# Low parts of weight blocks made 2048 columns at a time, a fourth row pair in sevens, and modulations moved out of a matrix

## The chip, the cores and the metric

The kernel runs on one core of one Trainium2 chip. The metric is the device time of the whole program in microseconds (us), the median of several runs. A core has five engines that run on their own and wait for each other by semaphores: TensorE (PE, matrix products into the eight banks of PSUM), VectorE (DVE), ScalarE (ACT), GpSimd (POOL), and SyncE (SP), which here issues the loads.

## The reference

A trunk of two layers over 256 tokens of width 2048, all in fp32. Each layer has a token mixer and a SwiGLU feed-forward; both are fed by an RMS norm with a shift and a scale, and added back through a gate. Shift, scale and gate are columns of a product of the conditioning vector with `w_mod` (the modulations):

```python
for i in range(DEPTH):                       # 2 layers
    mod = (c_act @ w_mod[i] + b_mod[i])[:, None, :]
    sh1, sc1, g1, sh2, sc2, g2 = jnp.split(mod, 6, axis=-1)
    h = rms_norm(x, norm1_g[i]) * (1.0 + sc1) + sh1
    y = retention_mixer(h, ...) if i == 0 else short_conv_mixer(h, ...)
    x = x + g1 * y
    h = rms_norm(x, norm2_g[i]) * (1.0 + sc2) + sh2
    a, b = jnp.split(h @ ffn_w_in[i], 2, axis=-1)      # 2048 -> 2 x 5632
    x = x + g2 * ((jax.nn.silu(a) * b) @ ffn_w_out[i]) # 5632 -> 2048
return rms_norm(x, final_g)
```

## The kernel before

**Products in parts.** An fp32 weight `w` and an activation are each written as a high and a low part that TensorE takes at full rate, and a product is three matmuls (high x high, high x low, low x high). ScalarE makes the high part by a cast (L419), VectorE the low part by subtracting the high part from the raw weight (L422).

**Blocks, pieces and places.** All weight matrices lie in one array `w_all` of 456 blocks of 128 rows x 2048 columns, in the order of their use. A block is loaded into one of four buffers `raw` (1 MB a load; the modulations' rows of `w_mod` take the same four buffers). `prepare` handles one piece of a block at a time: piece 0 and piece 1 are the two halves of 1024 columns. Each piece goes to the next of five places (`PLACES`) of 1024 columns in the tiles `hi` and `lo`; they are used in turn, so a cast into a place must wait until TensorE has read what stood there five places ago. `take` hands weights to the matmuls and calls `prepare` whenever a place has been used up and `fits()` says that there is room.

**Sevens.** In the first matrices of the feed-forwards, eight row pairs (two rows of 128 each, one block: two rows times two groups of 512 columns) make one group of 512 x 2 output columns for 256 tokens. A plain row pair takes 24 matmuls of 512 columns. Some row pairs are done with seven products for eight (`Seven`, 21 matmuls): VectorE makes sums and differences of the block's quarters, in four pieces: piece 2 (difference of quarters into `differences`, then the low part of columns 1024 to 2047), piece 3 (low part of `differences`), piece 4 (one 512-wide difference, then the low part of columns 0 to 1023), piece 5 (one more 512-wide difference and its 512-wide low part). That is seven VectorE operations: four of 1024 columns and three of 512, and four casts. The activations of such a row pair are summed as well, once, in `made_in_sums`. At a group's end `mixed_sums` and `last_input` put the banks together on VectorE (ten operations of 512), and a transposition, called two row pairs into the next group, adds two more. `FFN_SEVEN` names the row pairs of layer 0 that are sevens, `IN_SEVEN` and `OUT_SEVEN` those of layer 1. Layer 0's matrix is used in two parts: four such groups (after some first columns), its output matrix's first rows, then six such groups and the remaining output rows.

**Modulations.** There are 160 outside the start, each one load of 1 MB and one VectorE operation of 2048 columns (L326). `paced` spreads them over the program by `plan_mod`, a list of points (units of work done so far, modulations done by then); a unit is 128 x 128 weights. The retention mixer covers units 0 to 2048 (its first 496 in a form of its own, `RET_SPANS`), layer 0's feed-forward units 2048 to 4160: first columns and four groups to 2688, output to 3008, six groups to 3776, output to 4160; the convolution mixer ends at 5184.

**Order.** TensorE's instructions stand in the order in which the code is written. VectorE's and ScalarE's are put in order by a scheduler, and each engine then runs its list strictly from first to last: an instruction that waits holds up all behind it on its engine.

Of the kernel before, what the change touches and what calls it, by code (L numbers as in the profile page):

```python
# [31 lines left out]
CHUNK = 2048  # L32
HALF = 1024
# [8 lines left out]
IN_SEVEN, OUT_SEVEN, TURNS_AT, BESIDE_CB, BESIDE_SUMS = (3, 4, 6), ((2, 4, 6, 5, 1), (2, 4, 6, 10, 8)), 2, 40, 48  # L42
LAST_TILES = 20, 24
ONE_GROUP = (1, 1)
FFN_TILES, FFN_SEVEN, FFN_TURNS = (20, 24), (2, 4, 6), 2
STORE_AT, LOAD_AT = 0, 2
LEAD_RET, LEAD_CONV, LEAD_FFN = 6, 4, 2
AHEAD = 2
# [5 lines left out]
PLACES = 5  # L54
FETCHED, PLAIN, WARM, ADDED = 2, 3, (5, 0, 0, 0, 0, 0, 0, 8), ()
# [71 lines left out]
RET_SPANS, RET_HEADS = ret_in_groups()  # L127
# [6 lines left out]
class Seven:  # L134
# [6 lines left out]
    n = 2 * DV // P  # L141
# [123 lines left out]
def trunk(ctx: ExitStack, tc: tile.TileContext, x_in, c_in, pos_in, w_mod, cols_in, gain_in, tab_in, w_all, out):  # L265
    nc = tc.nc
    const = ctx.enter_context(tc.tile_pool(name="const", bufs=1))
    work = ctx.enter_context(tc.tile_pool(name="work", bufs=2))
    wpool = ctx.enter_context(tc.tile_pool(name="wpool", bufs=1))
# [22 lines left out]
    at = [0]  # L292
# [49 lines left out]
    n_mod = len(todo)  # L342
    todo.reverse()
    first = RET_SPANS[0].n * FIRST_KS
    early = sum(g.n * len(g.ks) for g in RET_SPANS)
    plan_mod = [(early, 0), (1024, 28), (1984, 72), (2688, 80), (3008, 96), (3776, 102), (5184, n_mod)]
    units, allowed = [0], [0.0]

    def paced(n):
# [19 lines left out]
    ready, place, raws, fetched, n_fetched = [], [None], [], {}, [0]  # L369
    in_seven, n = set(), 0  # L370
# [2 lines left out]
            in_seven.add(n // CHUNK)  # L373
        n += g.n * P * len(g.ks)

    pieces = [(i, p) for i in range(PLAIN, w_all.shape[0]) for p in ((2, 3, 4, 5) if i in in_seven else (0, 1))]

    def fetch():
        raw = wpool.tile([P, CHUNK], F32, tag="raw", name=name("raw"), bufs=RAW_BUFS)
# [13 lines left out]
    def prepare(between=None):  # L393
        if prepared[0] == len(pieces):
            return
        index, piece = pieces[prepared[0]]
        prepared[0] += 1
        if piece in (0, 2, 6):
            raws[:] = [next_raw(index)]
            while first <= units[0] < early and len(fetched) < RAW_BUFS - 1 and n_fetched[0] < w_all.shape[0]:  # L400
                fetch()
        whole = raws[0]
        b = [whole[:, i : i + DV] for i in range(0, CHUNK, DV)]
        raw = whole[:, :HALF] if piece in (0, 4) else whole[:, HALF:] if piece < 6 else whole
        if piece == 2:
            nc.vector.tensor_tensor(differences[0], whole[:, DV : 3 * DV], whole[:, : 2 * DV], op=ALU.subtract)
        elif piece == 3:
            raw = differences[0]
        elif piece == 4:
            nc.vector.tensor_tensor(b[1], b[2], differences[0][:, :DV], op=ALU.subtract)  # L410
        elif piece == 5:
            nc.vector.tensor_tensor(b[3], b[3], b[1], op=ALU.subtract)
            raw = b[3]
        width, at = raw.shape[1], HALF * (taken_places[0] % PLACES)
        taken_places[0] += -(-width // HALF)
        hi, lo = [t[:, at : at + width] for t in split_weights]
        steps = [slice(i, min(i + HALF, width)) for i in range(0, width, HALF)]
        for o in steps:
            nc.scalar.copy(hi[:, o], raw[:, o])  # L419
        if between:  # L420
            between()
        nc.vector.tensor_tensor(lo, raw, hi.bitcast(F32), op=ALU.subtract)  # L422
        ready.extend((hi[:, o], lo[:, o], o.stop - o.start) for o in steps)

    taken_places = [0]
    split_weights = [
        wpool.tile([P, PLACES * HALF], F32R, tag=tag, name=tag) for tag in ("hi", "lo")
    ]
    prepared = [0]

# [291 lines left out]
    with ExitStack() as inner:  # L722
# [64 lines left out]
        with tc.tile_pool(name="start", bufs=1) as sp:  # L787
# [59 lines left out]
            with tc.manual_schedule(engines={mybir.EngineType.DVE, mybir.EngineType.Activation}):  # L847
# [35 lines left out]
                sums = bank()[:, 0, :]  # L883
# [436 lines left out]
    with tc.tile_pool(name="ffn", bufs=1) as fpool:  # L1320
        h = rows_at(EARLIER)
        own.update(pool=fpool, sums={}, turns=FFN_TURNS)
        first_mid = paired(fpool, max(FFN_TILES))[: FFN_TILES[0] // 2]
        differences[0] = fpool.tile([P, 2 * DV], F32, tag="differences", name="differences")
        own["extra"] = [fpool.tile([P, DV], F32, tag=f"extra{i}", name=f"extra{i}") for i in range(2)]
        for part in range(2):
            n = FFN_TILES[part] // 2
            mid = paired(fpool, FFN_TILES[part]) if part else first_mid
            if not part:
                first_rows(FFN_FIRSTS, mid[-2:], 0, 1)  # L1330
                made_in_sums(FFN_SEVEN, [
                    fpool.tile([P, 2, P], F32R, tag=f"sums{i}", name=f"sums{i}") for i in range(6)
                ] + [tmp("u", (P, 2, P), F32R, bufs=3) for _ in range(3)])
# [13 lines left out]
    for i, g in enumerate(CONV_IN):  # L1347
        pending += [sums(g)] if i else normed(acc, 1, 0, g)
        while len(pending) >= 3:
# [3 lines left out]
            b, c, u = pb(tmp("bsum", pool=mpool, bufs=2)), pc(), pu()  # L1353
# [205 lines left out]
```

## Time and profile before

| | before |
|---|---|
| time, median of 3 runs (lowest to highest) | 2562.66 us (2562.12 to 2562.8) |
| span of the profiled execution, first to last instruction | 2558.4 us |
| granted TensorE clock | 0.998 |
| busy PE / VectorE / ScalarE | 2539.3 / 2354.7 / 1351.2 us |
| `lo` subtractions (L422) | 1062, of which 78 have 512 columns, the others 1024 |
| modulations outside the start (L326) | 160 |
| HBM read | 685.11 MB |

The profile is one execution; the page gives its span, and no time of its own beyond that. The span is 4.3 us below the median of the runs. Lines name kernel.py's lines of the kernel before. In a timeline row stand the start, the length (both us from the span's start), engine, line, operation, output <- inputs, shapes, and in brackets how long the engine was idle before and what ended that. Successive VectorE operations may overlap by their ends, so a step from start to start is shorter than the length.

### The profile page before, as it was taken

What the parts mean: (1) busy time and instruction counts of PE and PEld (TensorE: products, weight loads), DVE (VectorE), ACT (ScalarE), POOL (GpSimd) and SP (SyncE); (2) the same over time, 40 slices, a digit from 0 to 9 for tenths busy, and PEclk for the clock granted to TensorE, in tenths of its full rate; (3) what the DMA queues carried; (4) which work ended last, traced back from release to release, by engine and by line L of the source; (5) the groups of instructions that cost most, each with busy time, mean ns of one, the idle gap of its engine ahead of it and who ended that gap; (6) DMA issues with size and microseconds to landing.
All of it is one profiled execution on the core that took longest, in us unless ns stands there. A gap on an engine that the chain in (4) does not pass through costs nothing.

```text
span 2558.4 us, 34761 instructions
## 1 busy us (share of the span) xinstructions
PE 2539.3 (99%) x13237; PEld 2181.4 (85%) x13237; DVE 2354.7 (92%) x2968; ACT 1351.2 (53%) x1799; POOL 179.3 (7%) x234
## 2 busy tenths in 40 slices
PE   8999999999999999999999999999999999999998
PEld 7898888888889888888888898888998888888886
DVE  7989999898899999889999899888989999999998
ACT  5544543454456554345555454445566555555554
POOL 0000121011110001000000012000000000000001
PEclk9999999999999999999999999999999999999999
DMA  9987888879875667866667879888846465555653
GB/s 399 396 329 264 319 317 340 333 287 331 325 281 213 237 234 293 336 249 228 216 228 299 328 270 344 314 306 309 323 158 215 180 230 214 181 214 183 228 183 146
DMA packets 96695, 689.47 MB, mean 269 GB/s; under 512 B 10744, under 2 KB 12168, under 8 KB 13456
## 3 DMA queue, kind: packets, MB, share of 16 engines
q1 hardware_dynamic: 96528, 687.25, 72.2%
q8 instruction: 103, 1.69, 0.3%
q14 instruction: 64, 0.52, 0.1%
HBM read 685.11 MB, written 2.11 MB: 269 GB/s over the span
## 4 chain that ended last, share of the span: by engine, by line
PE 94%; DVE 3%; DMA 1%; ACT 1%; issue 1%; POOL 0%; SPq 0%; ACTq 0%; POOLq 0%; DVEq 0%
PE bank L472 22%; PE bank L487 17%; PE bank L485 17%; PE bank L486 17%; PE bank L475 11%; DVE lo L422 1%; PE bank L667 1%; PE bank L669 1%; PE bank L668 1%; PE bank L536 1%; PE bank L535 1%; PE bank L534 1%; DVE raw L798 1%; DMA raw<-w_all 1%; PE bank L1290 1%; PE bank L1067 1%
## 5 line engine op out<-in xcount | busy, mean ns | idle before, releaser
L419 ACT CAST hi<-raw 128x1024 fp32r<-128x1024 f32 (+1 forms) x984 | 991.1, 1019 | 936.7 <-PE bank L487 325.1
L422 DVE TENSOR_TENSOR lo<-raw,hi 128x1024 fp32r<-128x1024 f32 (+1 forms) x984 | 1143.3, 1179 | 125.6 <-ACT hi L419 116.7
L485 PE MATMUL bank<-hi,h 128*128 128x512 f32 x1540 | 602.9, 391 | 0.0
L487 PE MATMUL bank<-hi,h 128*128 128x512 f32 x1540 | 601.2, 390 | 0.0
L486 PE MATMUL bank<-lo,h 128*128 128x512 f32 x1540 | 601.1, 390 | 0.0
L326 DVE SCALAR_TENSOR_TENSOR raw<-raw,cb 128x2048 f32<-128x2048 f32 x160 | 365.4, 2285 | 8.2 <-DMA raw<-w_mod 8.0
L472 PE MATMUL bank<-h,hi 128*128 128x512 f32 x1012 | 352.8, 392 | 0.0
L487 PEld LDWEIGHTS bank<-hi,h 128*128 128x128 f32 x1540 | 289.4, 188 | 61.0
L485 PEld LDWEIGHTS bank<-hi,h 128*128 128x128 f32 x1540 | 289.6, 188 | 58.1
L486 PEld LDWEIGHTS bank<-lo,h 128*128 128x128 f32 x1540 | 289.7, 188 | 57.5
L472 PE MATMUL bank<-mid,hi 128*128 128x512 f32 x920 | 319.4, 391 | 0.0
L475 PE MATMUL bank<-h,lo 128*128 128x256 f32 x1012 | 285.0, 282 | 0.0
L475 PE MATMUL bank<-mid,lo 128*128 128x256 f32 x920 | 259.7, 282 | 0.0
L472 PEld LDWEIGHTS bank<-h,hi 128*128 128x128 f32 x1012 | 190.1, 188 | 40.3
L472 PEld LDWEIGHTS bank<-mid,hi 128*128 128x128 f32 x920 | 172.9, 188 | 35.6
L475 PEld LDWEIGHTS bank<-h,lo 128*128 128x128 f32 x1012 | 191.6, 189 | 0.5
L475 PEld LDWEIGHTS bank<-mid,lo 128*128 128x128 f32 x920 | 174.3, 189 | 0.1
L472 PE MATMUL bank<-rm,hi 128*128 128x512 f32 x496 | 172.5, 391 | 0.0
L475 PE MATMUL bank<-rm,lo 128*128 128x256 f32 x496 | 140.0, 282 | 0.0
L487 PE MATMUL bank<-hi,mid 128*128 128x512 f32 x284 | 110.9, 391 | 0.0
L485 PE MATMUL bank<-hi,mid 128*128 128x512 f32 x284 | 110.9, 391 | 0.0
L486 PE MATMUL bank<-lo,mid 128*128 128x512 f32 x284 | 110.7, 390 | 0.0
(300 smaller groups left out, 3344.2 us busy)
## 6 DMA issues: line engine op xcount, KB each, us to landing
raw<-w_all SPq DMA_DIRECT2D x456, 1024.0 KB, 5.0
raw<-w_mod SPq DMA_DIRECT2D x192, 1024.0 KB, 6.1
x<-x_in SPq DMA_DIRECT2D x4, 512.0 KB, 5.3
out<-xt SPq DMA_DIRECT2D x4, 512.0 KB, 3.0
decay<-tab_in SPq DMA_DIRECT2D x8, 128.0 KB, 4.9
x<-gate_row SPq DMA_DIRECT2D x2, 512.0 KB, 4.6
last_gain<-gain_in SPq DMA_DIRECT2D x1, 1024.0 KB
cols<-cols_in SPq DMA_DIRECT2D x1, 152.0 KB, 8.2
```

The costliest lines, as they stand in the source:

```text
L326: nc.vector.scalar_tensor_tensor(raw, raw, 1.0, cb, op0=ALU.mult, op1=ALU.mult, accum_out=total)
L419: nc.scalar.copy(hi[:, o], raw[:, o])
L422: nc.vector.tensor_tensor(lo, raw, hi.bitcast(F32), op=ALU.subtract)
L472: nc.tensor.matmul(pt, hi, h, start=fresh and k == g.ks[0], stop=False, skip_group_check=True)
L475: nc.tensor.matmul(pt[:, 1, :], lo, h[:, 0, :], start=False, stop=last and k == g.ks[-1], skip_group_check=True)
L485: nc.tensor.matmul(o, hi, w_hi, start=first, stop=False)
L486: nc.tensor.matmul(o, hi, w_lo, start=False, stop=False)
L487: nc.tensor.matmul(o, lo, w_hi, start=False, stop=last)
L534: nc.tensor.matmul(pt, hi, h[:, 0, :], start=first, stop=False, skip_group_check=True)
L535: nc.tensor.matmul(pt, hi, h[:, 1, :], start=False, stop=False, skip_group_check=True)
L536: nc.tensor.matmul(pt, lo, h[:, 0, :], start=False, stop=last, skip_group_check=True)
L667: nc.tensor.matmul(pt, hi, high, start=k == 0, stop=False, skip_group_check=True)
```

## The change

Three things change.

1. Blocks that are neither in sevens nor among the first 31 blocks (and the one behind them) are prepared as one piece, number 6: two casts of 1024 columns into two places as before, and then one subtraction of 2048 columns for both. Where the two places are the last and the first, the second lies four places back, and the operation takes them with a negative step. There are 336 such blocks. `fits()` lets such a piece be prepared only when two of the five places are free.
2. `FFN_SEVEN` goes from row pairs (2, 4, 6) to (2, 3, 5, 6). Ten groups each have one more seven, and `made_in_sums` makes a fourth set of sums.
3. `plan_mod`: 32, not 28, modulations by unit 1024; 78, not 72, by 1984; still 80 by 2688 and 96 by 3008; then 96, not 102, by 3776: none during the six groups, and six more after them.

```diff
-FFN_TILES, FFN_SEVEN, FFN_TURNS = (20, 24), (2, 4, 6), 2
+FFN_TILES, FFN_SEVEN, FFN_TURNS = (20, 24), (2, 3, 5, 6), 2
...
-    plan_mod = [(early, 0), (1024, 28), (1984, 72), (2688, 80), (3008, 96), (3776, 102), (5184, n_mod)]
+    plan_mod = [(early, 0), (1024, 32), (1984, 78), (2688, 80), (3008, 96), (3776, 96), (5184, n_mod)]
...
-    pieces = [(i, p) for i in range(PLAIN, w_all.shape[0]) for p in ((2, 3, 4, 5) if i in in_seven else (0, 1))]
+    apart = range(sum(g.n * len(g.ks) for g in RET_SPANS) * P // CHUNK + 1)
+    pieces = [(i, p) for i in range(PLAIN, w_all.shape[0]) for p in ((2, 3, 4, 5) if i in in_seven else (0, 1) if i in apart else (6,))]
...
-        nc.vector.tensor_tensor(lo, raw, hi.bitcast(F32), op=ALU.subtract)
-        ready.extend((hi[:, o], lo[:, o], o.stop - o.start) for o in steps)
+        if n == 1:
+            nc.vector.tensor_tensor(los[0], raw, his[0].bitcast(F32), op=ALU.subtract)
+        else:
+            step = 1 if at + 1 < PLACES else 1 - PLACES
+            end = None if at + 2 * step < 0 else at + 2 * step
+            hi, lo = [t[:, at:end:step, :] for t in split_weights]
+            raw = raw.rearrange("p (a b) -> p a b", a=2)
+            nc.vector.tensor_tensor(lo, raw, hi.bitcast(F32), op=ALU.subtract)
+        ready.extend((hi, lo, v.shape[1]) for hi, lo, v in zip(his, los, rows))
...
-        wpool.tile([P, PLACES * HALF], F32R, tag=tag, name=tag) for tag in ("hi", "lo")
+        wpool.tile([P, PLACES, HALF], F32R, tag=tag, name=tag) for tag in ("hi", "lo")
...
-                    fpool.tile([P, 2, P], F32R, tag=f"sums{i}", name=f"sums{i}") for i in range(6)
+                    fpool.tile([P, 2, P], F32R, tag=f"sums{i}", name=f"sums{i}") for i in range(9)
```

The lists below are of the second of the six groups. A block's name `raw_N` stands for one row pair. Before, `raw_9787` is row pair 3 (plain), `raw_9805` row pair 4 (seven), `raw_9851` row pair 5 (plain), `raw_9869` row pair 6 (seven). ScalarE before:

```order
L1294 CAST mid_9413<-bank_9776 128x2x256
L419 CAST hi<-raw_9787 128x1024
L419 CAST hi<-raw_9805 128x1024
L419 CAST hi<-differences 128x1024
L419 CAST hi<-raw_9805 128x1024
L419 CAST hi<-raw_9805 128x512
L419 CAST hi<-raw_9851 128x1024 x2
L419 CAST hi<-raw_9869 128x1024
```

After, `raw_9675` is row pair 3 (now a seven), `raw_9715` row pair 4 (plain), `raw_9726` row pair 5 (seven), `raw_9772` row pair 6 (seven), `raw_9812` row pair 7. ScalarE after, the same stretch:

```order
L1303 CAST mid_9306<-bank_9664 128x2x256
L421 CAST hi<-differences 128x1024
L421 CAST hi<-raw_9715 128x1024
L421 CAST hi<-raw_9675 128x1024
L421 CAST hi<-raw_9675 128x512
L421 CAST hi<-raw_9715 128x1024
L421 CAST hi<-raw_9726 128x1024
```

Before, a seven's casts stand together and the next plain block's two behind them; now the plain block's first cast (`raw_9715`) stands ahead of the seven's last two (`raw_9675`). At row pairs 6 and 7 it stands ahead of the 512-wide one:

```order
L421 CAST hi<-raw_9772 128x1024
L421 CAST hi<-differences 128x1024
L421 CAST hi<-raw_9772 128x1024
L421 CAST hi<-raw_9812 128x1024
L421 CAST hi<-raw_9772 128x512
L421 CAST hi<-raw_9812 128x1024
```

Over the ten groups the first of these places occurs ten times and the second nine times; in layer 1, of 37 places where a plain block follows a seven, twice each. VectorE before, from the same group:

```order
L422 TENSOR_TENSOR lo<-raw_9805,hi 128x512
L406 TENSOR_TENSOR differences<-raw_9869 128x1024
L326 SCALAR_TENSOR_TENSOR raw_9691,msum_9693<-raw_9691,cb 128x2048
L422 TENSOR_TENSOR lo<-raw_9851,hi 128x1024 x2
L422 TENSOR_TENSOR lo<-raw_9869,hi 128x1024
```

and after:

```order
L413 TENSOR_TENSOR raw_9675<-raw_9675 128x512
L407 TENSOR_TENSOR differences<-raw_9726 128x1024
L425 TENSOR_TENSOR lo<-raw_9675,hi 128x1024
L425 TENSOR_TENSOR lo<-raw_9675,hi 128x512
L431 TENSOR_TENSOR lo<-raw_9715,hi 128x2048
L425 TENSOR_TENSOR lo<-raw_9726,hi 128x1024
```

The modulation (L326) has left the group, and the plain row pair's two low parts are one operation (L431).

More of the change, by code (lines that the diff above doesn't have):

```diff
@@ L413, in prepare @@
             raw = b[3]
[L414 to L419, printed above, removed]
+        width, at = raw.shape[1], taken_places[0] % PLACES
+        n = -(-width // HALF)
+        taken_places[0] += n
+        rows = [raw[:, i : min(i + HALF, width)] for i in range(0, width, HALF)]
+        his, los = [[t[:, (at + i) % PLACES, : v.shape[1]] for i, v in enumerate(rows)] for t in split_weights]
+        for hi, v in zip(his, rows):
+            nc.scalar.copy(hi, v)
         if between:
             between()
-        nc.vector.tensor_tensor(lo, raw, hi.bitcast(F32), op=ALU.subtract)
-        ready.extend((hi[:, o], lo[:, o], o.stop - o.start) for o in steps)
+        if n == 1:
[7 more added lines that the diff above has]
+        ready.extend((hi, lo, v.shape[1]) for hi, lo, v in zip(his, los, rows))
     taken_places = [0]
     split_weights = [
-        wpool.tile([P, PLACES * HALF], F32R, tag=tag, name=tag) for tag in ("hi", "lo")
+        wpool.tile([P, PLACES, HALF], F32R, tag=tag, name=tag) for tag in ("hi", "lo")
     ]
```

## The prediction

> **What bounds the kernel now.** I read the page first (busy time, then the chain that ended last), then the groups of instructions by shape, the windows by stage, and last the timelines of single row pairs.
>
> ```profile
> span 2558.4 us, 34761 instructions
> PE 2539.3 (99%) x13237; PEld 2181.4 (85%) x13237; DVE 2354.7 (92%) x2968; ACT 1351.2 (53%) x1799; POOL 179.3 (7%) x234
> PE 94%; DVE 3%; DMA 1%; ACT 1%; issue 1%; POOL 0%; SPq 0%; ACTq 0%; POOLq 0%; DVEq 0%
> L485 PE MATMUL bank<-hi,h 128*128 128x512 f32 x1540 | 602.9, 391 | 0.0
> L422 DVE TENSOR_TENSOR lo<-raw,hi 128x1024 fp32r<-128x1024 f32 x906 | 1096.0, 1221 | 124.8 <-ACT hi L419 115.9 <-PE bank L472 2.5
> L326 DVE SCALAR_TENSOR_TENSOR raw<-raw,cb 128x2048 f32<-128x2048 f32 x160 | 365.4, 2285 | 8.2 <-DMA raw<-w_mod 8.0
> L419 ACT CAST hi<-raw 128x1024 fp32r<-128x1024 f32 x906 | 946.3, 1053 | 899.5 <-PE bank L487 324.8 <-PE bank L472 291.4 <-DMA raw<-w_all 109.6
> L419 ACT CAST hi<-raw 128x512 fp32r<-128x512 f32 x78 | 48.5, 621 | 37.3 <-DVE raw L412 36.1 <-PE bank L487 0.3 <-DVE x L406 0.3
> ```
>
> TensorE carries 94% of the chain and its matmuls of 512 columns waited 0.0 us, so its count of matmuls is worth time one for one. VectorE is second at 92%. ScalarE's casts idle 899.5 us, mostly until PE has let go of a place. In the stages that the change touches (the windows' columns are the stretch, its length, then each engine's busy time):
>
> ```profile
> 200.00:300.00 100.00, 99.46 (x510) 84.68 (x509) 99.13 (x137) 51.17 (x76) 11.79 (x14) 1.00 0.79 297
> 300.00:400.00 100.00, 100.00 (x533) 86.40 (x532) 95.30 (x130) 44.47 (x64) 21.65 (x26) 1.00 0.84 319
> 988.00:1099.00 111.00, 111.00 (x645) 98.66 (x644) 98.12 (x109) 43.76 (x44) 9.00 (x17) 1.00 0.87 330
> 1141.60:1184.20 42.60, 42.60 (x193) 35.18 (x192) 40.43 (x46) 24.28 (x27) 1.11 (x1) 1.00 0.62 223
> ```
>
> The last row is one group of the first feed-forward matrix (eight row pairs, three in sevens, one modulation): PE 42.6 of 42.6 us, VectorE 40.4. The two rows at the top are the retention heads, the third a feed-forward output.
>
> The row that decides is how a seven meets the next plain block. PE, ScalarE and VectorE at such a meeting (start, length):
>
> ```profile
> 1110.61 0.39 PE L487 MATMUL bank<-hi,h 128*128 128x512 f32 x1
> 1110.84 0.39 PE L485 MATMUL bank<-hi,u 128*128 128x512 f32 x1
> ...
> 1113.78 0.39 PE L486 MATMUL bank<-lo,h 128*128 128x512 f32 x1
> ...
> 1115.14 0.39 PE L486 MATMUL bank<-lo,h 128*128 128x512 f32 x1
> ...
> 1115.82 0.39 PE L486 MATMUL bank<-lo,h 128*128 128x512 f32 x1
> 1108.61 1.05 ACT L419 CAST hi<-raw 128x1024 fp32r<-128x1024 f32 x1 [0.68 <-DVE raw L410]
> 1111.08 2.52 ACT L419 CAST hi<-raw 128x1024 fp32r<-128x1024 f32 x3 [1.43 <-PE bank L487]
> 1110.15 1.23 DVE L422 TENSOR_TENSOR lo<-raw,hi 128x1024 fp32r<-128x1024 f32 x1
> 1112.17 2.96 DVE L422 TENSOR_TENSOR lo<-raw,hi 128x1024 fp32r<-128x1024 f32 x3 [0.79 <-ACT hi L419]
> ```
>
> PE begins a seven at s = 1110.84. ScalarE had stood idle 1.43 us at the cast of the next plain block's first place, which is the fifth after the last place of the row pair in front; it starts at 1111.08, s+0.24. The seven's own last cast (512 wide) stands behind it in ScalarE's queue. VectorE, idle 0.79 us for the same cast, makes the plain low part first (to 1113.39, read at 1115.82), then the 512 one (to 1113.99, read at 1115.14: 1.15 us to spare). The seven's third piece is read at 1113.78 = s+2.94; here it stood ahead of the waiting cast, its low part ended at 1111.38, and nothing was lost.
>
> **Durations.** PE's step is 0.2265 us (20 from 1110.61 to 1115.14). VectorE's steps, back to back:
>
> ```profile
> 1163.92 2.28 DVE L326 SCALAR_TENSOR_TENSOR raw<-raw,cb 128x2048 f32<-128x2048 f32 x1
> 1166.13 0.08 DVE L326 DVE_READ_ACCUMULATOR raw<-raw,cb 128x1 f32 x1
> 1166.13 3.49 DVE L422 TENSOR_TENSOR lo<-raw,hi 128x1024 fp32r<-128x1024 f32 x3
> 1143.02 0.68 DVE L1276 TENSOR_TENSOR u<-bank,u 128x512 f32<-128x512 f32 x1
> 1143.61 0.68 DVE L1276 TENSOR_TENSOR extra<-bank,extra 128x512 f32<-128x512 f32 x1
> 1152.56 1.03 PE L1290 MATMUL bank<-tab,extra 128*128 128x128 f32 x8
> 1195.20 1.04 PE L1290 MATMUL bank<-tab,extra 128*128 128x128 f32 x8
> ```
>
> Three of 1024 last 3.49, so a step is (3.49-1.22)/2 = 1.135; 512 steps 0.60; 2048 steps 2.21 (nearest row: the modulation's, the only 2048-wide operation). A wide low part has no row. 0.60 and 1.135 make 0.535 for 512 columns and 0.065 fixed, so 2048 take 2.205; the modulation says 2.21, and the ends are 2.14 (no fixed part) and 2.27 (two of 1024). I take a step of 2.20 and a length of 2.28. It saves 0.07 us a block, 336 blocks, 23 us of VectorE, hidden behind PE wherever PE is the bound: 0.
>
> **The fourth seven.** Ten groups each lose 24-21 = 3 matmuls: 30 x 0.2265 = 6.8 us of PE, on the path: **-6.8**. VectorE's work in a group becomes 16 operations of 1024 (18.2), 24 of 512 with the twelve of the group's end (14.4), four wide (8.8) = 41.4 us without waits; PE's is 42.64-0.68 = 41.96 (a group repeats after 1195.20-1152.56 = 42.64). Taking the group's modulation out (2.2) is what makes this fit; it alone buys nothing, as PE hid it. So VectorE has 0.5 us of room in 42.
>
> **What the order does at row pairs 3 and 4.** In the changed order ScalarE casts the first place of plain row pair 4 *ahead of* the third and fourth piece of the seven of row pair 3 (all ten groups). That place is freed when PE ends row pair 2, at s of row pair 3. With the measured chain: cast s+0.24, the third piece's cast 0.95 later, s+1.19 to 2.24, its low part s+2.28 to 3.50. PE wants it at s+2.94, so it waits 0.6 us. Then the 512 low part (s+3.42) and the wide one, s+4.02 to 6.30 (its second cast is done at s+3.7). PE wants that at s+4.79+0.23+0.60 = 5.62: 0.7 more. Together 1.35 us a group, x10 = **+13.5**. Behind the waiting cast stand the next casts, behind those every low part of VectorE, which has no room to make it up.
>
> **Wide after a seven elsewhere.** From the second layer, the seven at 2285.48 and the plain block after it:
>
> ```profile
> 2285.48 0.39 PE L485 MATMUL bank<-hi,u 128*128 128x512 f32 x1
> 2290.47 0.39 PE L486 MATMUL bank<-lo,h 128*128 128x512 f32 x1
> 2285.72 1.05 ACT L419 CAST hi<-raw 128x1024 fp32r<-128x1024 f32 x1 [1.13 <-issue]
> 2287.09 1.06 ACT L419 CAST hi<-raw 128x1024 fp32r<-128x1024 f32 x1 [0.32 <-PE bank L487]
> 2286.81 3.95 DVE L422 TENSOR_TENSOR lo<-raw,hi 128x1024 fp32r<-128x1024 f32 x3 [0.88 <-ACT hi L419]
> ```
>
> Now the first low part ends at 2288.03, 2.44 before it is read (2290.47). A wide one needs both casts, 2288.15, and ends at 2290.47: nothing left, some 0.06 us lost each time. In layer 1 the changed order has 37 such meetings: 33 plain (2.0), two with the cast ahead of the third piece (2.7), two with it ahead of the fourth (0.35 each, 0.7). At row pair 7 of the ten groups the 512 cast again stands behind the plain block's first, which puts its second cast 0.3 later: nine of 0.35 and one of 0.06, 3.2. Together **+8.6**, ends 3.4 (0.06 everywhere) and 14.
>
> **Modulations.** Six more run before the first feed-forward: 6 x 2.21 = 13.3 us of VectorE, less 97 blocks x 0.07 = 6.8 saved there. VectorE is 97% busy from 200 to 400 us by the windows. The worst lead there, in the first retention output:
>
> ```profile
> 411.42 2.35 DVE L422 TENSOR_TENSOR lo<-raw,hi 128x1024 fp32r<-128x1024 f32 x2
> 413.82 0.28 PE L475 MATMUL bank<-rm,lo 128*128 128x256 f32 x1
> 405.62 2.01 ACT L419 CAST hi<-raw 128x1024 fp32r<-128x1024 f32 x2 [2.95 <-DMA raw<-w_all]
> ```
>
> The first low part ended at 412.64, 1.2 before use; the wide form ends 1.1 later, at the edge. ScalarE stood 2.95 us for a load, so a late load is also felt about 2 us more (the second cast and the longer subtraction). Between 0 and 13; I take **+2**, nearest to the single edge that the row shows. One modulation is left in the first part's third group, and the first group makes a fourth set of sums: 0 to 4.4, **+1**, as that group loses two modulations. Six later ones go where VectorE has 12% free (98.1 of 111 in the like stage): 0. DMA counts and bytes stay; the queue only moves.
>
> Sum: -6.8+13.5+8.6+2+1 = **+18.3**. The profiled span is 2558.4, 4.3 below the median of 2562.66; the median plus the sum is **2581**.
>
> Of VectorE's steps: rows 1166.13 and 1143.02 show operations that start 0.086 us before the one in front has ended. The Trainium skill's page VectorE: DVE Perf Modes says otherwise in its section on the DRAIN: the next operation starts only when the pipe has emptied (it adds that one that is not held starts earlier). Its errata section gives an fp32 tensor_tensor (N+151)/0.96 ns, 1224 for 1024 columns; the trace's length of 1221 agrees, its step of 1135 does not. By that rule the time would be the first rival's.
>
> **Rivals.**
> *VectorE becomes the bound outright.* If operations did not overlap, a group would be 16 x 1.221 + 24 x 0.687 + 4 x 2.285 = 45.2 us against 42.64, ten times 2.5 = 25, with 9 for the rest: **2597**. The three in 3.49 us speak against it; so does a group before, whose 22 operations of 1024, 21 of 512 and one modulation would need 43.7 by lengths yet show 40.43. 0.07.
> *The waits are covered* (the other side). If the casts at row pair 3 came 0.6 us earlier, by a shorter cast or a freed place, and VectorE's 41.4 stayed under 41.96, only the 6.8 us of PE remain: **2556**. It decides where waits fall below 0.68 us a group. The third piece had such a cover before, by its place in the queue, and the 1.15 us at 1115.14 are one; nothing frees the place sooner. 0.10.
> *The mixer loses more.* The six modulations find no gaps and loads come late: +11 on top, **2592**. For it 99.13 of 100 us; against it PE's 99.46 there, and slack in most blocks. 0.10.
> *Half of the stalls.* Row pair 4 catches up, only 0.6 and 0.06 remain: -6.8+6.6+3 = +3, **2565**; VectorE's room of 0.5 would have to serve it. With less in the rest this is no change. 0.13.
>
> **How the numbers follow.** My forecast has 0.60, own range 2571 to 2592 (row pair 4 half caught up, the rest at its low ends; the rest at its high ends). Within 0.2% (5.1 us, about what a measurement tells apart) lies the half-stall case, 0.13; faster only the covered one, 0.10; the rest, 0.77, is slower. Leaving out the covered case, the range is 2563 to 2597.
>
> **What would show it.** The matmuls of L485 to L487 fall by 30 and no longer have idle 0.0; VectorE's `lo` appears 336 times as one 2048-wide operation of 2.28 us; the repeat of a feed-forward group grows from 42.6 to about 43.6; PE waits some 0.6 us for `lo` in the middle of row pair 3's seven and 0.7 at row pair 4, with ScalarE idle until PE at a cast of plain `raw` just ahead. I am wrong if the repeat is 42.0, or if VectorE is busy throughout a group and PE's waits lie all over it.

## The result and the profile after

The changed kernel takes 2606.97 us (median of 4 runs, 2604.09 to 2608.53) against 2562.39 us (2560.7 to 2562.8): a ratio of 1.0176, 95% interval 1.0161 to 1.019. It is slower, as forecast, but by 44.6 us and not by 18.3, and outside the range (2563 to 2597). The profiled execution took 2607.33 us. From its page, the span, the busy times, the chain by engine, and two groups (operation, count, busy time, mean ns, idle time in front and what ended it):

```profile
span 2605.6 us, 34376 instructions
PE 2560.5 (98%) x13207; PEld 2173.6 (83%) x13207; DVE 2371.7 (91%) x2692; ACT 1365.2 (52%) x1823; POOL 188.4 (7%) x234
PE 81%; DVE 13%; issue 4%; ACT 2%; DMA 0%; POOL 0%; ACTq 0%; POOLq 0%; DVEq 0%
L431 DVE TENSOR_TENSOR lo<-raw,hi 128x2048 fp32r<-128x2048 f32 x336 | 768.0, 2286 | 94.6 <-ACT hi L421 93.7
L495 PE MATMUL bank<-lo,h 128*128 128x512 f32 x1500 | 591.3, 394 | 16.6 <-DVE lo L425 8.6
```

PE has its 30 matmuls less. VectorE's share of the chain grew from 3% to 13% though VectorE is busy 91% of the span, not more than before: over the whole span no other engine became the bound, PE waits here and there for a low part. So the question is at which places. The table splits the span at matmuls that stand in both kernels (the first matmul of each normed product, and the transposition behind each feed-forward group); differences to before in us, one profiled execution each. "Ten groups" are the first feed-forward's four groups and, with its output rows between, the six up to the last transposition.

| kernel | mixer | first four groups | six groups | outputs, convolution | layer 1, first rows | layer 1, rest | span |
|---|---|---|---|---|---|---|---|
| before, us | 771.8 | 221.8 | 366.7 | 485.8 | 102.6 | 609.5 | 2558.4 |
| after | +14.8 | +9.8 | +6.2 | 0.0 | +1.2 | +15.2 | +47.2 |
| predicted | +2 | +5 | +6 | 0 | 0 | +5.4 | +18.3 |

The prediction's terms for the ten groups (-6.8, +13.5, 3.2, +1) make 10.9; they are parted here as four to six.

### The profile page after: what moved, and what is told of

The parts are those of the page before. It is cut to its first block, busy times and chain, and to the rows that moved or that the text cites. A ratio compares the mean times of both kernels' runs of the same rounds, so it can differ in the third digit from the quotient of the medians.

```text
span 2605.6 us, 34376 instructions
## 1 busy us (share of the span) xinstructions
PE 2560.5 (98%) x13207; PEld 2173.6 (83%) x13207; DVE 2371.7 (91%) x2692; ACT 1365.2 (52%) x1823; POOL 188.4 (7%) x234
## 4 chain that ended last, share of the span: by engine, by line
PE 81%; DVE 13%; issue 4%; ACT 2%; DMA 0%; POOL 0%; ACTq 0%; POOLq 0%; DVEq 0%
PE bank L481 20%; PE bank L495 14%; PE bank L496 14%; PE bank L494 13%; PE bank L484 11%; DVE lo L431 4%; DVE lo L425 3%; ACT hi L421 2%; PE bank L544 1%; PE bank L545 1%; PE bank L543 1%; PE bank L676 1%; PE bank L678 1%; PE bank L677 1%; DVE raw L326 1%
## 5 line engine op out<-in xcount | busy, mean ns | idle before, releaser
L431 DVE TENSOR_TENSOR lo<-raw,hi 128x2048 fp32r<-128x2048 f32 x336 | 768.0, 2286 | 94.6 <-ACT hi L421 93.7
L495 PE MATMUL bank<-lo,h 128*128 128x512 f32 x1500 | 591.3, 394 | 16.6 <-DVE lo L425 8.6
L494 PE MATMUL bank<-hi,h 128*128 128x512 f32 x1500 | 587.8, 392 | 0.7 <-ACT hi L421 0.7
L496 PE MATMUL bank<-hi,h 128*128 128x512 f32 x1500 | 586.1, 391 | 0.0
L425 DVE TENSOR_TENSOR lo<-raw,hi 128x512 fp32r<-128x512 f32 (+1 forms) x322 | 340.8, 1074 | 40.1 <-ACT hi L421 38.0
L326 DVE SCALAR_TENSOR_TENSOR raw<-raw,cb 128x2048 f32<-128x2048 f32 x160 | 365.1, 2283 | 3.7 <-DMA raw<-w_mod 3.1
L495 PEld LDWEIGHTS bank<-lo,h 128*128 128x128 f32 x1500 | 282.4, 188 | 91.3 <-DVE lo L431 22.6
L494 PEld LDWEIGHTS bank<-hi,h 128*128 128x128 f32 x1500 | 282.4, 188 | 58.8 <-ACT hi L421 1.4
L496 PEld LDWEIGHTS bank<-hi,h 128*128 128x128 f32 x1500 | 282.0, 188 | 58.3
L496 PE MATMUL bank<-hi,mid 128*128 128x512 f32 x284 | 110.9, 391 | 0.0
```

The source lines that it names most:

```text
L326: nc.vector.scalar_tensor_tensor(raw, raw, 1.0, cb, op0=ALU.mult, op1=ALU.mult, accum_out=total)
L425: nc.vector.tensor_tensor(los[0], raw, his[0].bitcast(F32), op=ALU.subtract)
L494: nc.tensor.matmul(o, hi, w_hi, start=first, stop=False)
L495: nc.tensor.matmul(o, hi, w_lo, start=False, stop=False)
L496: nc.tensor.matmul(o, lo, w_hi, start=False, stop=last)
```

## The experiments

All kernels below are told by the same table:

| kernel | mixer | first four groups | six groups | outputs, convolution | layer 1, first rows | layer 1, rest | span |
|---|---|---|---|---|---|---|---|
| wide low parts alone | +3.6 | +5.5 | +2.6 | +1.6 | +0.8 | +15.3 | +29.4 |
| plan alone | +9.2 | +1.0 | +0.6 | 0.0 | +2.5 | -0.2 | +13.0 |
| sevens and plan, halves | +6.6 | +2.8 | +3.5 | 0.0 | +5.6 | -0.2 | +18.3 |
| after, halves behind sevens | +12.1 | +5.8 | +5.0 | 0.0 | +0.3 | +3.6 | +26.8 |
| sevens 2, 4, 5, 6 | +0.9 | 0.0 | -2.1 | +10.1 | +4.1 | -0.2 | +12.8 |
| sevens 2, 3, 5, 6 | +2.1 | +1.9 | -0.1 | +10.5 | +3.8 | -0.2 | +18.0 |
| after, halves in the mixer | +7.0 | +9.4 | +6.3 | +1.4 | +1.2 | +15.9 | +41.2 |
| plan, later in the mixer | +5.1 | +1.5 | +0.5 | +0.9 | +3.9 | -0.2 | +11.7 |
| sevens alone | +0.9 | +13.2 | +6.5 | +0.2 | 0.0 | +0.5 | +21.2 |
| 2, 4, 5, 6, eight modulations late | +0.2 | 0.0 | -2.1 | +0.2 | +21.7 | -0.2 | +19.7 |
| 2, 4, 5, 6 in the six groups | +0.3 | 0.0 | -1.4 | +0.2 | +4.3 | -0.2 | +3.2 |

In the mixer some 2 us vary between executions of kernels that are alike there ("sevens 2, 4, 5, 6" and "2, 3, 5, 6": +0.9 and +2.1). It is the start that varies: at 186 us, ahead of the first wide low part (204.9 us in after), after stands at +2.7 already, "plan alone" at +2.8 and "2, 3, 5, 6" at +2.1, all others at +0.2 to +0.9.

### One part of the change alone

**Wide low parts alone**: after, with three sevens and the plan of before.

```diff
-FFN_TILES, FFN_SEVEN, FFN_TURNS = (20, 24), (2, 3, 5, 6), 2
+FFN_TILES, FFN_SEVEN, FFN_TURNS = (20, 24), (2, 4, 6), 2      # and six sums
-    plan_mod = [(early, 0), (1024, 32), (1984, 78), (2688, 80), (3008, 96), (3776, 96), (5184, n_mod)]
+    plan_mod = [(early, 0), (1024, 28), (1984, 72), (2688, 80), (3008, 96), (3776, 102), (5184, n_mod)]
```

> Only the 2048-wide low parts, with the sevens and the modulations of before. If the two-place low part itself is what costs (it can start only when two places are free): layer 1 stays some 17 us longer as in the changed kernel, the mixer keeps most of its 15, a feed-forward group with three sevens loses a little at each plain block behind a seven; 2585 to 2600 us. If the fourth seven and the moved modulations are what costs, VectorE has 23 us less to do and nothing waits longer: 2555 to 2563 us.

Measured: 2589.43 us, ratio 1.0113 (1.0098 to 1.0128). All of layer 1's loss is here, three times what was predicted, and 8.1 us of the ten groups'. A layer 1 meeting in the timelines of after (start, length; in brackets the idle time in front and what ended it):

```profile
1993.50 1.05 ACT L421 CAST hi<-raw 128x1024 fp32r<-128x1024 f32 x1 [0.17 <-PE bank L496]
...
1993.30 1.22 DVE L407 TENSOR_TENSOR x<-raw 128x1024 f32<-128x1024 f32 x1
1994.55 0.69 DVE L411 TENSOR_TENSOR raw<-raw,x 128x512 f32<-128x512 f32 x1
1995.16 2.28 DVE L431 TENSOR_TENSOR lo<-raw,hi 128x2048 fp32r<-128x2048 f32 x1
...
1996.65 0.39 PE L494 MATMUL bank<-hi,h 128*128 128x512 f32 x1
1997.50 0.50 PE L495 MATMUL bank<-lo,h 128*128 128x512 f32 x1 [0.47 <-DVE lo L431]
```

The plain block's second cast ends at 1994.55. VectorE spends the wait on the *next* seven's differences (L407), and then its L411 stands in front too: the wide low part starts 0.61 after the cast. PE's matmuls start 0.85 apart instead of 0.23, so this one is 0.62 late, and the matmul behind it (1997.84) another 0.11. In halves the first low part needs only the first cast.

Not every meeting is like this one. Layer 1 has 36 such waits, at 34 meetings, in after as in this kernel. At 14 meetings PE loses 0.26 to 1.2 us, at two of these 1.1 and then 0.6 more (there the cast order is turned round as well); in seven of the 14 the next seven's L407 and L411 stand directly in front of the wide low part. At the other 20 PE loses 0.04 to 0.06. The matmul behind is 0.11 late each time, however long the wait was. The waits make 11.5 us, the matmuls behind them 4.0. One of the 20 is the meeting that the prediction priced (2285.48 before). VectorE and PE there, in after:

```profile
2286.63 2.29 DVE L431 TENSOR_TENSOR lo<-raw,hi 128x2048 fp32r<-128x2048 f32 x1 [2.68 <-ACT hi L421]
...
2288.98 0.50 PE L495 MATMUL bank<-lo,h 128*128 128x512 f32 x1
2289.32 0.39 PE L496 MATMUL bank<-hi,h 128*128 128x512 f32 x1
```

VectorE has nothing else to do there and starts 0.03 after the second cast has ended (2286.60). PE's steps are 0.29 and 0.34.

**Halves behind sevens**: after, where a block right behind a seven is prepared in halves.

```diff
-... if i in apart else (6,))]
+... if i in apart or i - 1 in in_seven else (6,))]
```

> The changed kernel, with the block directly behind a seven made in halves again (all others wide). If the waits in layer 1 and at row pair 4 are those of a two-place low part right behind a seven, layer 1 is back within 3 us of before, a group of layer 0 repeats after about 42.5, and what is left is the mixer's 15: 2575 to 2580 us. If it is VectorE's load, this adds about 4 us of work to VectorE and the whole stays at 2605 us or above.

Measured: 2586.69 us, ratio 1.01 (1.0085 to 1.0115). Layer 1 falls from 16.4 to 3.9, so the loss there is that of wide low parts behind sevens: it is the place, not the width, that costs. The six groups stay at +5.0, which was not expected: instead of waits of 0.55 and 0.62 there is one of 1.47, because the plain low part's first half now also stands ahead of the seven's third piece. So this run does not show what the wide low part alone costs in a group.

**Plan alone**: before, with the changed list of points.

```diff
-    plan_mod = [(early, 0), (1024, 28), (1984, 72), (2688, 80), (3008, 96), (3776, 102), (5184, n_mod)]
+    plan_mod = [(early, 0), (1024, 32), (1984, 78), (2688, 80), (3008, 96), (3776, 96), (5184, n_mod)]
```

> Only the modulations moved (28 to 32, 72 to 78, 102 to 96). If six more modulations overfill VectorE in the mixer, the mixer is 10 to 15 us longer and the whole 2572 to 2577 us. If the wide low parts are what makes the mixer longer, this is 2562 to 2565 us.

Measured: 2573.41 us, ratio 1.0048 (1.0031 to 1.0064). The plan takes six modulations out of the first four groups into the mixer, and six out of the six groups to behind unit 3776. Neither place gains by it (+1.0 and +0.6). The mixer loses about 6.4 us (9.2 with the varying start), the convolution nothing, layer 1's first rows 2.5. A place in the mixer, in the timelines of this kernel, with PE's last:

```profile
335.54 2.28 DVE L326 SCALAR_TENSOR_TENSOR raw<-raw,cb 128x2048 f32<-128x2048 f32 x1
...
337.75 2.28 DVE L326 SCALAR_TENSOR_TENSOR raw<-raw,cb 128x2048 f32<-128x2048 f32 x1
...
339.96 2.28 DVE L326 SCALAR_TENSOR_TENSOR raw<-raw,cb 128x2048 f32<-128x2048 f32 x1
...
342.17 2.35 DVE L422 TENSOR_TENSOR lo<-raw,hi 128x1024 fp32r<-128x1024 f32 x2
...
343.44 0.49 PE L486 MATMUL bank<-lo,h 128*128 128x512 f32 x1 [0.90 <-DVE lo L422]
```

Three modulations in a row hold VectorE for 6.6 us. They also share the four `raw` buffers with the weights. From the waits between 330 and 400 us (who <- for whom: us in total, times, longest) of this kernel:

```profile
ACT hi L419 <- DMA raw<-w_all: 30.0, 8, 5.8
```

and of before:

```profile
ACT hi L419 <- DMA raw<-w_all: 11.7, 4, 4.2
```

ScalarE waits 30.0 us for the weights' loads instead of 11.7. How much of the mixer's loss is VectorE's time and how much the later loads, no run parts.

**Sevens and plan, halves everywhere**: before, with the changed row pairs and plan.

```diff
-FFN_TILES, FFN_SEVEN, FFN_TURNS = (20, 24), (2, 4, 6), 2
+FFN_TILES, FFN_SEVEN, FFN_TURNS = (20, 24), (2, 3, 5, 6), 2
(the plan as in "plan alone"; nine sums)
```

> Fourth seven and moved modulations, all low parts in halves of 1024. If the cast order at row pair 3 costs 0.6 us whatever the width, and the 0.6 at row pair 4 is the wide low part's, a group repeats after about 42.5 us (42.64 - 0.68 + 0.6) and the whole is 2560 to 2565 us. If VectorE has no room for a fourth seven, its groups stay at 43.6 or more, having lost the saving of the wide ones, and the whole is 2570 us or more.

Measured: 2578.0 us, ratio 1.0066 (1.0051 to 1.0081). A group of the six repeats after 42.88 us (before 42.63): one wait of about 0.74, with the 0.11 behind it, eats the 0.68 that the seven saves, and more. The wait is at the third piece of row pair 3's seven. So the fourth seven gains nothing even without wide low parts.

**Sevens alone**: the same with before's plan.

> Before with the four sevens 2, 3, 5, 6 and nothing else: halves everywhere, before's plan, so about two modulations in each of the first part's groups and one in each of the six. Theory (VectorE full: 41.7 us a group without a modulation and 2.2 for each, against 41.96 of PE): a group of the six repeats after about 43.9 instead of 42.64, five of them +6, the first part's groups after 44 to 46, +6 to 14, mixer 0: 2573 to 2583. Rival (only the order of casts costs, 0.74 us a group as with the modulations moved away): FFN +3 to 6, mixer 0: 2563 to 2567.

Measured: 2582.26 us, ratio 1.0083 (1.0069 to 1.0096). A group repeats after 43.85 to 43.87 us, as VectorE's 41.7 + 2.2 say. The modulation's place in the timelines:

```profile
1172.86 2.29 DVE L326 SCALAR_TENSOR_TENSOR raw<-raw,cb 128x2048 f32<-128x2048 f32 x1
...
1175.07 1.22 DVE L422 TENSOR_TENSOR lo<-raw,hi 128x1024 fp32r<-128x1024 f32 x1
...
1176.35 0.50 PE L486 MATMUL bank<-lo,h 128*128 128x512 f32 x1 [0.54 <-DVE lo L422]
```

Here VectorE is the bound: it is busy 43.85 of the 43.85 us from 1178.00 to 1221.85. With a modulation in the group a fourth seven costs 1.2 us; without one, 0.25.

### The order of casts or VectorE's load

**Sevens 2, 4, 5, 6** and **sevens 2, 3, 5, 6**: four sevens, halves, no modulation in any of the ten groups, the mixer's plan as before. The two differ in one number.

```diff
-FFN_TILES, FFN_SEVEN, FFN_TURNS = (20, 24), (2, 4, 6), 2
+FFN_TILES, FFN_SEVEN, FFN_TURNS = (20, 24), (2, 4, 5, 6), 2      # the other: (2, 3, 5, 6); both with nine sums
-    plan_mod = [..., (1984, 72), (2688, 80), (3008, 96), (3776, 102), (5184, n_mod)]
+    plan_mod = [..., (1984, 72), (2688, 72), (3008, 88), (3776, 88), (5184, n_mod)]
```

> Before with four sevens at row pairs 2, 4, 5, 6 (all low parts in halves), and no modulation in any of the ten groups (72 by unit 2688, 88 from 3008 to 3776, so 14 more behind them); the mixer's plan is that of before. In its order a plain block's first cast stands ahead of the third piece of the seven in front once in ten groups, not ten times. Theory (the stall belongs to that order of casts, and VectorE's 16+8 operations of 1024 and 24 of 512, 41.7 us a group, just fit): the group repeats after 41.96 us, -6.8 in all; +1 to 2 for the fourth set of sums in the first group, +3 to 6 in layer 1's first rows, where the plans with more late modulations lost 2.5 and 5.6: 2557 to 2561, about 2559. Rival (VectorE is simply full with a fourth seven): a group of 42.4 us or more, so 2563 or more.

> The same as the kernel with sevens at row pairs 2, 4, 5, 6, but with the changed kernel's row pairs 2, 3, 5, 6: the same number of operations on every engine, another place of one seven. In its order the plain block's first cast stands ahead of the third piece of row pair 3's seven in eight groups. Theory (order of casts): one PE wait of 0.6 to 0.75 us in each of the eight, so about 5 to 6 us more than with 2, 4, 5, 6: 2562 to 2567. Rival (VectorE's load decides): the same time for both, within 2 us.

Measured: 2573.37 us, ratio 1.0048 (1.0036 to 1.0061), and 2576.61 us, ratio 1.0059 (1.0047 to 1.0072). Both lie above what was expected, and their intervals overlap; the traces part the two. With row pair 3 PE waits there in the eight groups whose casts stand so, 0.73 to 0.74 us in seven and 1.56 in the first; with row pair 4 only in the first, 1.30 us, the one group whose casts stand so. The groups of the second part repeat after 42.88 us (42.08 in the one without the wait) and 42.34 us. ScalarE, VectorE and PE of the kernel with row pair 3:

```profile
1203.91 4.41 ACT L419 CAST hi<-raw 128x1024 fp32r<-128x1024 f32 x5 [2.36 <-PE bank L487]
...
1205.00 4.10 DVE L422 TENSOR_TENSOR lo<-raw,hi 128x1024 fp32r<-128x1024 f32 x4 [0.28 <-ACT hi L419]
...
1207.42 0.50 PE L486 MATMUL bank<-lo,h 128*128 128x512 f32 x1 [0.58 <-DVE lo L422]
```

ScalarE stands 2.36 us until PE lets go of a place, for the plain block's cast; the seven's casts stand behind it in the run of five. This is the mechanism that the prediction priced, by itself. But a group of "2, 4, 5, 6", without it, repeats after 42.34, not 41.96: of 0.68 us only 0.3 arrive. VectorE is busy 207.3 of 210 us there (199.0 before), by the window of 1140 to 1350 us (PE, PEld, VectorE, ScalarE, GpSimd):

```profile
1140.00:1350.00 210.00, 210.00 (x935) 171.62 (x934) 207.30 (x239) 127.45 (x145) 0.00 (x0) 1.00 0.53 197
```

Most of what is missing stands at one place in each group, just behind the group's end:

```profile
1186.44 0.50 PE L485 MATMUL bank<-hi,h 128*128 128x512 f32 x1
```

This matmul starts 0.38 after the one in front instead of 0.23, and 0.05 after the end of VectorE's L1224 (1185.70, 0.69 long), the last operation of `mixed_sums` in the order of VectorE, between low parts. The matmul behind it is again 0.11 late: 0.27 of the missing 0.38. That it waits for the bank which L1224 reads is the likely reading; no run tests it.

The groups gain 2.1 us with row pair 4, and the convolution loses 10, where the plan puts 72 modulations behind unit 3776 in place of 58. From the timelines of "2, 4, 5, 6":

```profile
1578.76 2.28 DVE L326 SCALAR_TENSOR_TENSOR raw<-raw,cb 128x2048 f32<-128x2048 f32 x1
...
1581.96 1.00 DVE L1360 SCALAR_TENSOR_TENSOR y<-cu,cols,y 128x256 f32<-128x256 f32 x2 [0.58 <-ACT y L1358]
1582.90 2.36 DVE L422 TENSOR_TENSOR lo<-raw,hi 128x1024 fp32r<-128x1024 f32 x2
...
1584.18 0.39 PE L475 MATMUL bank<-h,lo 128*128 128x256 f32 x1 [0.49 <-DVE lo L422]
```

### Where modulations may go

**Plan, later in the mixer**: before, with the mixer's six more behind unit 1024.

```diff
-    plan_mod = [(early, 0), (1024, 28), (1984, 72), (2688, 80), (3008, 96), (3776, 102), (5184, n_mod)]
+    plan_mod = [(early, 0), (1024, 28), (1984, 78), (2688, 80), (3008, 96), (3776, 96), (5184, n_mod)]
```

> Before with the six extra modulations of the mixer all between units 1024 and 1984 (28 by 1024 as before, 78 by 1984), the other points as changed. Theory (what costs is the rate in the stretch that ends at unit 1024, 0.061 a unit against 0.053, where the loads of raw blocks and of modulations share four buffers; the rate here is 0.052): the waits at 342 to 394 us are gone, the mixer loses 0 to 3, and with 2.5 at layer 1's first rows it is 2561 to 2566. Rival (six more operations of VectorE cost the mixer some 1 us each wherever they stand): the mixer loses 6 to 9, 2570 to 2573.

Measured: 2572.56 us, ratio 1.0042 (1.0029 to 1.0056). The waits between 342 and 394 us are gone, and others stand at 470, 524, 760 and 766 us. So the rate of the first stretch was not the cause: the mixer loses about 5 us to six modulations here and 6.4 as the change places them.

**Halves in the mixer**: after, with the mixer's blocks in halves.

```diff
-    apart = range(sum(g.n * len(g.ks) for g in RET_SPANS) * P // CHUNK + 1)
+    apart = range(2048 * P // CHUNK)
```

> The changed kernel with its blocks of the whole retention mixer (units 0 to 2048) in halves; its plan of modulations stays. Theory (the mixer loses to the modulations and to the wide low parts, both): the mixer falls from +14.8 to what the plan alone cost, 6.6 to 9.2 (two executions), so 2599 to 2601. Rival A (the modulations alone): it stays at 2607. Rival B (the wide low parts alone): the mixer is back at 0, 2592.

Measured: 2601.25 us, ratio 1.0159 (1.0143 to 1.0175). The mixer falls by 7.8 to what the plan costs. Of the 7.8 some 2.4 are the varying start; the other 5.4 go with the wide low parts. After's retention output, from VectorE's, ScalarE's and PE's timelines:

```profile
405.77 2.28 DVE L431 TENSOR_TENSOR lo<-raw,hi 128x2048 fp32r<-128x2048 f32 x1
407.97 2.28 DVE L326 SCALAR_TENSOR_TENSOR raw<-raw,cb 128x2048 f32<-128x2048 f32 x1
...
410.96 0.48 DVE L723 SCALAR_TENSOR_TENSOR sum<-bank,g,x 128x256 f32<-128x256 f32 x1 [0.70 <-PE bank L484]
...
411.88 2.28 DVE L431 TENSOR_TENSOR lo<-raw,hi 128x2048 fp32r<-128x2048 f32 x1
...
406.87 2.00 ACT L421 CAST hi<-raw 128x1024 fp32r<-128x1024 f32 x2 [3.64 <-DMA raw<-w_all]
...
414.22 0.38 PE L484 MATMUL bank<-rm,lo 128*128 128x256 f32 x1 [0.30 <-DVE lo L431]
```

and VectorE's at the same place with halves there:

```profile
405.70 0.48 DVE L723 SCALAR_TENSOR_TENSOR sum<-bank,g,x 128x256 f32<-128x256 f32 x1
...
408.89 2.29 DVE L326 SCALAR_TENSOR_TENSOR raw<-raw,cb 128x2048 f32<-128x2048 f32 x1
...
411.10 0.48 DVE L723 SCALAR_TENSOR_TENSOR sum<-bank,g,x 128x256 f32<-128x256 f32 x1
...
412.02 2.35 DVE L425 TENSOR_TENSOR lo<-raw,hi 128x1024 fp32r<-128x1024 f32 x2
```

After's second cast ended at 408.87, but the low part waits for 411.88: the column's end (L723) stands ahead of it and itself waits for PE, and PE then waits 0.46 for the low part. Each holds the other up once a column, and the column repeats after 6.11 us (PE's seven waits of 0.33 to 0.46 from 396 to 433 us). In halves the first half needs one cast only, no wait is left on VectorE, and the column repeats after 5.40 us (405.70 to 411.10; in before after 5.55).

**Sevens 2, 4, 5, 6, eight modulations late**:

```diff
-    plan_mod = [..., (3776, 88), (5184, n_mod)]
+    plan_mod = [..., (3776, 88), (5184, 152), (6912, n_mod)]
```

> The kernel with sevens 2, 4, 5, 6 and no modulation in the ten groups, with eight of the modulations taken out of the convolution and spread over layer 1's feed-forward instead (152 by unit 5184, the rest by 6912). Theory (an added modulation costs only where VectorE has less room than it takes: the convolution lost nothing with 58 and, in the changed kernel, with 64 behind unit 3776, and 9.9 us with 72; layer 1's feed-forward has VectorE free for 5 us in 100, 17.7 us for the eight): the convolution falls from +9.9 to 0 to 3, the rows behind it from +4 to 1 to 3, layer 1 gives 0 to 4 back: 2558 to 2566. Rival (a modulation costs 0.7 to 1 us wherever it stands): what the convolution gains layer 1 loses, 2570 to 2574.

Measured: 2580.89 us, ratio 1.0078 (1.0064 to 1.0091). With 64 modulations the convolution's 9.9 us are gone, as expected. But I had overlooked that layer 1's start asks for the last gate's modulations: all eight came within 23 us, seven of them in one run, and PE stood 18.45 us.

```profile
1858.93 2.29 DVE L326 SCALAR_TENSOR_TENSOR raw<-raw,cb 128x2048 f32<-128x2048 f32 x1
...
1872.24 2.29 DVE L326 SCALAR_TENSOR_TENSOR raw<-raw,cb 128x2048 f32<-128x2048 f32 x1
...
1875.77 0.58 PE L667 MATMUL bank<-h,hi 128*128 128x258 f32 x1 [18.45 <-ACT hi L419]
```

So what modulations cost in layer 1's groups was not tried.

**2, 4, 5, 6 in the six groups alone**, with their six modulations behind unit 3776, the version that the runs pointed to:

```diff
-FFN_TILES, FFN_SEVEN, FFN_TURNS = (20, 24), (2, 4, 6), 2
+FFN_TILES, FFN_SEVEN, FFN_TURNS = (20, 24), ((2, 4, 6), (2, 4, 5, 6)), 2      # by part
-    plan_mod = [..., (3008, 96), (3776, 102), (5184, n_mod)]
+    plan_mod = [..., (3008, 96), (3776, 96), (5184, n_mod)]
+            if part:
+                made_in_sums((5,), ...)
```

> Before with a fourth seven (row pairs 2, 4, 5, 6) in the six groups of the second part alone, its fourth sums made at that part's start, halves everywhere, and the six modulations of those groups behind unit 3776 (96 by 3776, so 64 behind it); the first part keeps three sevens and its modulations, the mixer its plan. Theory (a fourth seven pays where its order of casts leaves no wait and its group has no modulation, and the convolution takes 64 modulations without loss): five groups gave 1.7 us and the sixth some 0.3 with these row pairs, the fourth sums cost 0 to 1.5, layer 1's first rows 0 to 2.5: 2557 to 2562, about 2560, no difference that can be measured. Rival (six moved modulations cost 0.7 to 1 us each wherever they go): 2563 to 2567.

Measured: 2563.68 us against 2561.27, ratio 1.0008 (0.9999 to 1.0017): no difference that can be told, and no gain. The groups gain 1.4 to 2, and layer 1's first rows lose 4.3, of which a single wait is half:

```profile
1856.05 0.71 PE L593 MATMUL bank<-tab,rs 128*128 128x128 f32 x4 [1.91 <-POOL rs L586]
```

Behind this wait the granted clock is 0.50 from 1856.93 to 1860.34 us, and PE's steps are longer there; that is most of the other half. No version tried beats the kernel before.

## Why the prediction was right and wrong

The span grew by 47.2 us where the sum had 18.3. Of the difference the mixer has 12.8, layer 1 11.0, the first four groups 4.8.

**Right: the group.** The repeat was to grow from 42.6 to 43.6, with waits of 0.6 in row pair 3's seven and 0.7 at row pair 4, behind a cast that idles. In after (PE, ScalarE, VectorE):

```profile
1178.27 1.03 PE L1299 MATMUL bank<-tab,extra 128*128 128x128 f32 x8
1221.91 1.04 PE L1299 MATMUL bank<-tab,extra 128*128 128x128 f32 x8
...
1187.51 0.50 PE L495 MATMUL bank<-lo,h 128*128 128x512 f32 x1 [0.39 <-DVE lo L425]
...
1190.32 0.50 PE L495 MATMUL bank<-lo,h 128*128 128x512 f32 x1 [0.46 <-DVE lo L431]
...
1184.19 4.42 ACT L421 CAST hi<-raw 128x1024 fp32r<-128x1024 f32 x5 [2.37 <-PE bank L496]
...
1186.23 1.83 DVE L425 TENSOR_TENSOR lo<-raw,hi 128x1024 fp32r<-128x1024 f32 x2
1187.97 2.29 DVE L431 TENSOR_TENSOR lo<-raw,hi 128x2048 fp32r<-128x2048 f32 x1
```

The repeat is 43.64. The rows' matmuls start 0.55 and 0.62 later than PE's step allows (the brackets count from the end of the matmul in front, which otherwise reaches 0.16 into the next). The six groups lost 6.2, predicted 6. That the repeat fits so closely is partly luck: the two waits make 1.17 and not 1.35, row pair 7 loses 0.05 and not 0.35, and what fills the gap was not in the sum, 0.11 at the matmul behind each of the three. The two kernels that differ in one row pair show the cause of the wait in row pair 3's seven: a cast that waits for a place, ahead of casts that need not. The wait at row pair 4 stands in the rows as priced, but no run takes it away alone.

**Right: durations, and where nothing happens.** The wide low part lasts 2286 ns (predicted 2.28) and its step is 2.20 us (405.77 to 407.97 above); outputs and convolution lost 0.

**Wrong: "Wide after a seven elsewhere".** The term had 0.06 us a meeting, because the wide low part would start when its second cast ends. At the meeting that was priced, and at 19 others of layer 1, this is what came, with 0.11 more at the matmul behind. What failed is the step from this one row to all meetings: it needs VectorE free at the end of the second cast, and at 14 of 34 meetings VectorE was not, or the cast itself came late. In the row 1995.16 the next seven's L407 and L411 fill the wait for the cast and reach 0.61 beyond it. Waits of 11.5 and 4.0 behind them make 15.5 us; the wide low parts alone lost 16.1 in layer 1, where the term had 5.4. The row that I priced from showed VectorE idle 0.88 before the *first* cast; the question was what VectorE would do between the first and the second, at each meeting.

**Wrong: "Modulations".** +2 in the mixer became +14.8, of which 2.7 are the varying start. Six more cost about 6.5 (6.6, 9.2 and 7.0 in three executions, with 0.3, 2.8 and 0.3 of start), where the 13.3 us of VectorE's time less 6.8 were to fit almost wholly into gaps. The wide low parts were to give back these 6.8; a kernel with them alone lost 3.6 there, 0.9 of it start, so they gave nothing back; together they made the column of 6.11 us. VectorE's 97% was read right, and then priced by one edge in one row. The rival "the mixer loses more", +11 on top, was that close; it held 0.10.

**Wrong: the first group.** The fourth sums had +1. The first four groups lost 9.8, not 5. In the first one VectorE's order stands the wide low part ahead of the seven's own third piece:

```profile
852.56 2.29 DVE L431 TENSOR_TENSOR lo<-raw,hi 128x2048 fp32r<-128x2048 f32 x1
854.77 1.82 DVE L425 TENSOR_TENSOR lo<-raw,hi 128x1024 fp32r<-128x1024 f32 x2
...
856.04 0.50 PE L495 MATMUL bank<-lo,h 128*128 128x512 f32 x1 [2.01 <-DVE lo L425]
```

A wide operation put ahead of one that is needed sooner holds it up by 2.2 us here, where a half would by 1.1. And the wait costs more than its length, by two windows of equal length behind it (columns as above, then granted clock, DMA share, GB/s):

```profile
856.41:859.82 3.41, 3.41 (x10) 2.63 (x9) 3.41 (x5) 1.26 (x2) 0.00 (x0) 0.50 0.97 384
859.82:863.23 3.41, 3.41 (x17) 2.82 (x16) 3.41 (x5) 1.46 (x2) 0.00 (x0) 1.00 0.58 223
```

At a granted clock of 0.50 PE starts 10 matmuls where it then starts 17, which is 1.6 us more. The first group lost 5.3 in all, the second 2.5, with one wait of 1.9 at 903.98, the two behind it 1.0 each. The part of the fourth sums alone is the smaller one: with halves and no modulations the first four groups came out even.

**The rivals.** VectorE did not lose its overlap: the modulation at 407.97 starts 0.08 before the wide low part has ended. The section on the DRAIN of the Trainium skill's page VectorE: DVE Perf Modes has the next operation wait for an empty pipe, and adds that one that is not held starts earlier; these rows show an earlier start. That VectorE is the bound outright came true only where a modulation stays in a group with four sevens. The fourth seven's cover ("the waits are covered") exists with the seven at row pair 4, but with VectorE busy 207.3 of 210 us only 0.3 of 0.68 us arrive. Small slips in the sums change nothing: 0.06 at each of the 47 meetings is 2.8, not 3.4, and the lengths of a group before add up to 43.6, not 43.7.

## What to carry to other kernels

An operation merged from two halves needs the last input of both and holds its engine until the second half is done. Price it not by its length but by asking, at each place where it stands in an in-order list, when its last input comes, what the list puts in between, and what that reads next. The Trainium skill's page VectorE: DVE Perf Modes says, in its section on the errata, that one large operation pays the fixed latency once and many small ones each time. The trace agrees (2.20 against 2 x 1.135 us). Here the 0.07 us saved cost 0.17 us at the mild meetings and 0.4 to 1.9 at the others, where half of the result was wanted early.

An engine that is 97% busy beside the bound has little room: six operations of 2.2 us, moved out of a stretch where they cost nothing, cost about 1 us each in the mixer. Six others cost nothing in the convolution, where VectorE was busy 90% (270.5 of 300 us, 1500 to 1800 in before).

One meeting read closely is one meeting. Before a price is taken times 37, the other meetings' neighbours in the same list are to be read too.

## What was not expected of the hardware

A plan that left VectorE the same work in the mixer, only later, lost nearly as much (5.1 against 6.6 to 9.2 us). The convolution took 64 modulations behind unit 3776 with a loss of 0 to 1.4 us and 72 with 9.9 us: six waits of 0.65 us and one of 2.2 at its start among them, so the step from free to costly is short.

A wait of PE of some 2 us can be followed by 3.4 us at a granted clock of 0.50: in after behind 2.01 us (at 856), in "2, 4, 5, 6" behind 2.03 at the convolution's start (1542.98 to 1546.39), in the last kernel behind 1.91 (at 1856). It does not always come: in "plan alone" a wait of 1.93 at the same place as the last left the clock at 1.00. So a wait near 2 us can cost more than its length, and not the same in each kernel.

Layer 1's 3.9 us that halves behind sevens did not take back (five waits, the longest 1.64 us at 2565) were not traced further.
